# Attention's value projection: two of its four L21+L22 weight sums are added by DMA at pages 4 and 6 instead of by VectorE, and the loads and sums around them are placed anew

## The chip, the cores and the metric

The kernel runs on one core of a Trainium2 chip. The metric is the device time of one execution in microseconds (us); the median of three executions of the kernel before is 2254.22 us (2251.8 to 2255.15).

## The reference, cut to what matters

One layer of a streaming encoder on a sequence of 512 tokens of 2048 features, all in float32. What is touched here is one sixth of the input projection: the values of the attention heads, 512 x 2048 times 2048 x 1024.

```
h = rms_norm(x, norm_mix_w)
proj = h @ w_in                      # columns: q_a, k_a, v_a, q_g, k_g, v_g, r_g, gate_lr
y_a = chunked_band_attention(q_a, k_a, v_a, att_rel_bias)      # v_a: columns 2048 to 3071
y_g = rms_norm(gated_linear_attention(q_g, k_g, v_g, ...)) * silu(r_g)
x = x + concat(y_a, y_g) @ w_out
x = x + (gelu(conv(h2 @ w_ffn_up)[gate]) * conv(h2 @ w_ffn_up)[value]) @ w_ffn_down
x = x + sigmoid(h3 @ w_ple_gate) * (p @ w_ple_proj)
out = rms_norm(x, final_norm_w)
```

## The kernel before, in words

**The products.** Every large float32 product is cut in quarters and made with seven instead of eight quarter products (Strassen's scheme in Winograd's form). Each operand is split in a high part that a matmul takes whole and a low rest, and three matmuls (high x high, high x low, low x high) replace one float32 product. For the weights, a split is one ScalarE copy (the high part, `w`) and one VectorE subtraction (the low part, `w`), both of 128 x 1024.

**The values of attention** are the stage of this case. `values_product` (line 1140, called at line 1531) runs the seven products in the order P1, P2, P4, P5, P6, P3, P7, each over four weight pages j = 0 to 3 of 128 x 1024 (512 KB), so there are 28 pages, numbered n = 0 to 27. The weight operand of a page is

- pages 0 to 3: L11, 4 to 7: L12, 8 to 11: L22, each loaded as it lies in memory;
- pages 12 to 15: S1 = L21 + L22;
- pages 16 to 19: S2 = S1 + L11; pages 20 to 23: S4 = S2 + L12;
- pages 24 to 27: S3 = L21 + L11.

S1, S2 and S4 of one j are made one after the other in the same page of SBUF, named `wva_s0` to `wva_s3` in the program (`wva_s` in the profile). The pages that are loaded plainly, and those of S3, are named `wva_P..._r`: the first digit after P is the product, the second is j, so `wva_P40_r` is page 8 and `wva_P70_r` is page 24. They lie in a ring of four buffers, so page 24 takes the place of page 8, page 25 that of page 9, and so on.

**Four operations feed a page.** `value_load` (line 1112) and `sum_load` (line 1117) start a plain load from SyncE's queue, 16 and 4 of them, each 512 KB. `sum_more` (line 1121) starts a DMA from GpSimd's queue that adds a page of weights in memory onto a page in SBUF; "adding DMA" below. `sum_right` (line 1127) adds L22 onto a sum page by a VectorE instruction. `value_split` (line 1131) is the split; three buffers take its results in turn, so the split of page n + 2 is written in the program at page n and cannot begin before TensorE has left page n - 1.

**What sets the order.** At page n the program issues, in this order: the load of page n + 4 (while that is under 12), the split of page n + 2, then what the table at lines 1511 to 1522 lists for page n (`plan`), then the 12 matmuls of page n. After each product `values_collect` takes the result out of PSUM, on ScalarE or VectorE. From here on every engine and both DMA-issuing queues (SyncE's and GpSimd's) keep the order of the program (`in_order(True, True)`), so an instruction that waits holds up all that stands behind it on its engine. The other entries of the table are the last operands of this stage on the activation side (`right`, `differences`, `spread_differences`: ScalarE and VectorE), the output of the values before (`second_out`: ScalarE and GpSimd's queue), the forget gate of the linear attention (`gate_sum`, `gate_scan` on VectorE, `gate_decay` on ScalarE, `gate_small` on VectorE) and `give`, which hands a free page to the next stage, whose first weights are then loaded.

In the kernel before, L21 for the sums is loaded at pages 5 to 8, L22 is added by VectorE at pages 8 to 11, L11 by DMA at pages 11 to 14, L12 by DMA at pages 16 to 19. For S3, L21 is loaded at pages 9 to 12 and L11 added by DMA at pages 10, 15, 20 and 21.

The profile gives nearly all instructions line 64 (the helper that records them), so groups are told apart by tiles. The products' PSUM tiles are `vaA` to `vaD`: P1, P6 and P7 go to `vaA`, P2 to `vaB`, P4 to `vaD`, P5 and P3 to `vaC`.

Of the kernel before, what the change touches and what calls it, by code (L numbers as in the profile page):

```python
# [42 lines left out]
def encoder_block(ctx: ExitStack, tc: tile.TileContext, A, out):  # L43
# [1451 lines left out]
    va = dict(pages=[(p, j) for p in VALUE_ORDER for j in range(4)], raw={}, sum={}, l22={}, tiles={}, have=set())  # L1495

    def at_page(n, *fs):
        plan.setdefault(n, []).extend(fs)
# [10 lines left out]
        values_out(va["first"], 1, out_tiles, ts)  # L1509

    for n, *fs in ((0, (second_out, (0, 1)), (spread_differences, 4)),
                   (1, (second_out, (2, 3)), (right, 5), (right, 6)), (2, (differences, 5)), (3, (spread_differences, 5)), (4, (right, 7)),
                   (5, (sum_load, va, 0), (differences, 6)), (6, (sum_load, va, 1), (spread_differences, 6)),
                   (7, (sum_load, va, 2), (differences, 7)), (8, (sum_load, va, 3)), (9, (spread_differences, 7)),
                   (12, (gate_sum, (0, 1))), (13, (gate_scan, (0,))), (14, (gate_sum, (2, 3))), (15, (gate_scan, (1,))),
                   (16, (gate_scan, (2,))), (17, (gate_scan, (3,))),
                   *((8 + j, (sum_right, va, j)) for j in range(4)), *((9 + j, (value_load, va, 24 + j)) for j in range(4)),
                   *((11 + j, (sum_more, va, 16 + j, "L11")) for j in range(4)),
                   *((16 + j, (sum_more, va, 20 + j, "L12")) for j in range(4)),
                   *((i, (sum_more, va, 24 + j, "L11")) for j, i in enumerate((10, 15, 20, 21))),  # L1520
                   *((18 + i, (gate_decay, (i,))) for i in range(4)),
                   *((22 + i, (gate_small, (i,))) for i in range(4)), (26, (linear_pages,)),
                   *((n, (give, tag)) for n, tag in ((19, "r4"), (20, "r5"), (23, "r1"), (24, "r2"), (25, "r0"), (26, "r3")))):
        at_page(n, *(lambda f=f, a=a: f(*a) for f, *a in fs))
# [293 lines left out]
```

## Time and profile before

| | |
|---|---|
| three executions, median (lowest to highest) | 2254.22 us (2251.8 to 2255.15) |
| the profiled execution: its own time | 2254.77 us |
| the profiled execution: span, first to last instruction | 2253.1 us |
| mean granted TensorE clock | 0.998 |
| DMA traffic | 568.72 MB, mean 252 GB/s |

All times within the profile are microseconds from the start of the span. PE is TensorE, PEld its weight loads, DVE VectorE, ACT ScalarE, POOL GpSimd, SP SyncE; a name ending in q is an engine's queue of issues. "DMA share" is the mean busy share of the core's 16 DMA engines; it is a sum over queues and reads up to 1.06 to 1.08 when they are all busy. In a timeline the bracket at the end of a row tells how long the engine had been idle and what ended that. q1 is the DMA queue of SyncE's loads, q0 that of GpSimd's.

### The profile page before, as it was taken

How to read it: one execution, taken by the hardware profiler on the slowest of the kernel's cores; microseconds unless marked ns; L12 is line 12 of the kernel's file. 1: busy time of each engine (PE TensorE's matmuls, PEld its weight loads, DVE VectorE, ACT ScalarE, POOL GpSimd, SP SyncE). 2: the span in 40 equal slices, each digit the busy share in tenths (PEclk: the TensorE clock that was granted, in tenths of full speed). 3: DMA queues.
4: the chain of work that ended last, by engine and by line, in shares of the span. 5: the costliest groups of instructions: out<-in, count | busy, mean ns of one | idle time of the engine just before them, and what ended most of it. 6: DMA issues, size and time to landing. Idle time of an engine off the chain costs nothing.

```text
span 2253.1 us, 45666 instructions
## 1 busy us (share of the span) xinstructions
PE 2230.5 (99%) x18248; PEld 2180.2 (97%) x18248; DVE 1896.0 (84%) x2603; ACT 1321.7 (59%) x1960; POOL 199.2 (9%) x243
## 2 busy tenths in 40 slices
PE   9999999999999999999999999999999999999997
PEld 7879999999899999999999999999999999999997
DVE  6876779998688888898888888888898787898987
ACT  6654567776665665555555555555564554666765
POOL 1021111011100011111111100000000100000000
PEclk9999999999999999999999999999999999999999
DMA  5499889888978979999999987777866967879896
GB/s 206 131 238 252 223 228 241 235 229 239 355 260 246 341 211 291 289 279 285 281 265 284 260 235 209 218 208 215 263 227 220 317 212 234 309 246 335 280 296 207
DMA packets 202052, 568.72 MB, mean 252 GB/s; under 512 B 22032, under 2 KB 64272, under 8 KB 201840
## 3 DMA queue, kind: packets, MB, share of 16 engines
q1 hardware_dynamic: 168336, 448.58, 56.1%
q0 software_dynamic: 32064, 114.83, 27.2%
q8 instruction: 143, 2.34, 0.4%
q10 hardware_dynamic: 1440, 2.40, 0.3%
q14 instruction: 69, 0.57, 0.1%
HBM read 492.33 MB, written 119.54 MB: 272 GB/s over the span
## 4 chain that ended last, share of the span: by engine, by line
PE 89%; DVE 5%; DMA 3%; ACT 2%; issue 2%; POOL 0%; SPq 0%; DVEq 0%; ACTq 0%; POOLq 0%
PE accA L64 44%; PE accC L64 23%; PE accB L64 11%; PE v L64 4%; DVE w L64 2%; PE pp L64 1%; DMA wva_s<-in_w_v_a 1%; PE vaA L64 1%; PE py L64 1%; PE psc L64 1%; PE ptr L64 1%; DVE u L64 1%; PE po L64 1%; DVE s L64 1%; ACT w L64 1%
## 5 line engine op out<-in xcount | busy, mean ns | idle before, releaser
L64 PE MATMUL accA<-h,w 128*128 128x256 f32 x5088 | 628.7, 280 | 1.2 <-DVE w L64 0.7
L64 PEld LDWEIGHTS accA<-h,w 128*128 128x128 f32 x5088 | 608.9, 188 | 4.1 <-ACT u L64 1.1
L64 PE MATMUL accC<-h,w 128*128 128x256 f32 x4248 | 524.1, 280 | 0.8 <-DVE w L64 0.6
L64 DVE TENSOR_TENSOR w<-s,w 128x1024 fp32r<-128x1024 f32 (+1 forms) x381 | 457.1, 1200 | 77.7 <-ACT w L64 72.0
L64 PEld LDWEIGHTS accC<-h,w 128*128 128x128 f32 x4248 | 507.9, 188 | 1.5 <-DVE w L64 0.8
L64 ACT ACTIVATE w<-l 128x1024 fp32r<-128x1024 f32 (+1 forms) x320 | 331.8, 1038 | 186.8 <-PE accC L64 119.3
L64 DVE TENSOR_TENSOR w<-l,w 128x1024 fp32r<-128x1024 f32 (+1 forms) x320 | 382.4, 1195 | 58.1 <-ACT w L64 57.5
L64 ACT ACTIVATE w<-s 128x1024 fp32r<-128x1024 f32 (+1 forms) x381 | 394.9, 1037 | 39.1 <-DVE s L64 22.8
L64 ACT ACTIVATE u<-accA 128x256 f32<-128x256 f32 x302 | 114.4, 379 | 381.5 <-PE accA L64 381.3
L64 DVE TENSOR_TENSOR s<-s,l 128x1024 f32<-128x1024 f32 (+1 forms) x176 | 211.1, 1200 | 12.5 <-DMA s<-in_w_blk 9.3
L64 POOL DMA_DIRECT2D s<-in_w_up x84 | 74.1, 882 | 735.0 <-DMA s<-in_w_up 388.7
L64 DVE SCALAR_TENSOR_TENSOR cv<-u,cw,cv 128x511 f32<-128x511 f32 (+1 forms) x176 | 131.6, 748 | 3.1
L64 PE MATMUL accA<-up_R,w 128*128 128x256 f32 x1056 | 130.5, 280 | 0.0
L64 PE MATMUL accB<-up_R,w 128*128 128x256 f32 x1056 | 130.1, 279 | 0.0
L64 PE MATMUL accA<-up_N,w 128*128 128x256 f32 x1056 | 130.1, 279 | 0.0
L64 PEld LDWEIGHTS accA<-up_R,w 128*128 128x128 f32 x1056 | 126.1, 188 | 0.5 <-issue 0.5
L64 PEld LDWEIGHTS accB<-up_R,w 128*128 128x128 f32 x1056 | 126.1, 188 | 0.0
L64 PEld LDWEIGHTS accA<-up_N,w 128*128 128x128 f32 x1056 | 126.1, 188 | 0.0
L64 ACT ACTIVATE u<-accC 128x256 f32<-128x256 f32 x98 | 37.4, 382 | 92.0 <-PE accC L64 91.5
L64 DVE TENSOR_TENSOR u<-u,accC 128x256 f32<-128x256 f32 x102 | 42.7, 418 | 56.6 <-PE accC L64 55.4
L64 PE MATMUL v<-w,h 128*128 128x512 f32 x384 | 88.7, 391 | 0.9 <-ACT h L171 0.9
L64 PEld LDWEIGHTS v<-w,h 128*128 128x128 f32 x384 | 71.8, 188 | 16.6 <-ACT h L171 1.1
(302 smaller groups left out, 2900.2 us busy)
## 6 DMA issues: line engine op xcount, KB each, us to landing
l<-in_w_up SPq DMA_DIRECT2D x132, 512.0 KB, 6.9
s<-in_w_up SPq DMA_DIRECT2D x84, 512.0 KB, 6.0
s<-in_w_up POOLq DMA_DIRECT2D x84, 512.0 KB, 7.6
l<-in_w_dn SPq DMA_DIRECT2D x56, 448.0 KB, 5.0
l<-in_w_blk SPq DMA_DIRECT2D x48, 512.0 KB, 6.0
s<-in_w_blk SPq DMA_DIRECT2D x32, 512.0 KB, 4.6
s<-in_w_blk POOLq DMA_DIRECT2D x32, 512.0 KB, 7.8
l<-in_w_out SPq DMA_DIRECT2D x28, 512.0 KB, 4.4
```

What stands on the lines that cost most here:

```text
L64: ins = f(*args, **kw)
```

## The change

Only the table changes. Of the stage's sums:

- L22 of j = 0 and 1 is added by DMA (`sum_more` of pages 12 and 13, at pages 4 and 6) and not by VectorE; j = 2 and 3 stay on VectorE, at pages 10 and 11 as before. Two VectorE instructions go, two adding DMAs come.
- L21 for the sums is loaded at pages 1, 3, 5 and 7, not 5, 6, 7 and 8.
- L21 for S3 is loaded at pages 7, 8, 11 and 12, not 9, 10, 11 and 12.
- L11 is added onto it at pages 8, 9, 19 and 20, not 10, 15, 20 and 21.
- The adding DMAs of L12 (S4) stand at pages 15 to 18, not 16 to 19. Those of L11 for S2 stay at 11 to 14.

```diff
@@ -1509,15 +1509,17 @@
     for n, *fs in ((0, (second_out, (0, 1)), (spread_differences, 4)),
-                   (1, (second_out, (2, 3)), (right, 5), (right, 6)), (2, (differences, 5)), (3, (spread_differences, 5)), (4, (right, 7)),
-                   (5, (sum_load, va, 0), (differences, 6)), (6, (sum_load, va, 1), (spread_differences, 6)),
-                   (7, (sum_load, va, 2), (differences, 7)), (8, (sum_load, va, 3)), (9, (spread_differences, 7)),
+                   (1, (second_out, (2, 3)), (sum_load, va, 0), (right, 5), (right, 6)), (2, (differences, 5)),
+                   (3, (sum_load, va, 1), (spread_differences, 5)), (4, (right, 7), (sum_more, va, 12, "L22")),
+                   (5, (sum_load, va, 2), (differences, 6)), (6, (sum_more, va, 13, "L22"), (spread_differences, 6)),
+                   (7, (sum_load, va, 3), (differences, 7)), (9, (spread_differences, 7)),
...
-                   *((8 + j, (sum_right, va, j)) for j in range(4)), *((9 + j, (value_load, va, 24 + j)) for j in range(4)),
+                   (10, (sum_right, va, 2)), (11, (sum_right, va, 3)),
+                   *((i, (value_load, va, 24 + j)) for j, i in enumerate((7, 8, 11, 12))),
                    *((11 + j, (sum_more, va, 16 + j, "L11")) for j in range(4)),
-                   *((16 + j, (sum_more, va, 20 + j, "L12")) for j in range(4)),
-                   *((i, (sum_more, va, 24 + j, "L11")) for j, i in enumerate((10, 15, 20, 21))),
+                   *((15 + j, (sum_more, va, 20 + j, "L12")) for j in range(4)),
+                   *((i, (sum_more, va, 24 + j, "L11")) for j, i in enumerate((8, 9, 19, 20))),
```

**GpSimd's queue**, from the writes of P2's results (`vad`) on. Before, the S3 sum of page 24 stands ahead of the four sums with L11, and that of page 25 between them and the four sums with L12:

```order
L64 DMA vad_205<-pair_r6_106 128x4x128 x2
L64 DMA wva_P70_r_1198<-in_w_v_a 128x1024
L64 DMA wva_s0_1112<-in_w_v_a 128x1024
L64 DMA wva_s1_1134<-in_w_v_a 128x1024
L64 DMA wva_s2_1154<-in_w_v_a 128x1024
L64 DMA wva_s3_1178<-in_w_v_a 128x1024
L64 DMA wva_P71_r_1215<-in_w_v_a 128x1024
L64 DMA wva_s0_1112<-in_w_v_a 128x1024
```

The same place of the changed program, from two rows earlier:

```order
L64 DMA wva_s0_1033<-in_w_v_a 128x1024
L64 DMA wva_s1_1076<-in_w_v_a 128x1024
L64 DMA vad_205<-pair_r6_106 128x4x128 x2
L64 DMA wva_P70_r_1164<-in_w_v_a 128x1024
L64 DMA wva_P71_r_1184<-in_w_v_a 128x1024
L64 DMA wva_s0_1033<-in_w_v_a 128x1024
L64 DMA wva_s1_1076<-in_w_v_a 128x1024
L64 DMA wva_s2_1117<-in_w_v_a 128x1024
L64 DMA wva_s3_1158<-in_w_v_a 128x1024
L64 DMA wva_s0_1033<-in_w_v_a 128x1024
```

The two new sums stand ahead of P2's writes, and both early S3 sums stand ahead of the four sums with L11; nothing is left between these and the sums with L12. Behind the last sum with L12 come the S3 sums of pages 26 and 27 in both.

**SyncE's queue**, from the load of page 6 (`wva_P22_r`) on, before:

```order
L64 DMA wva_P22_r_1050<-in_w_v_a 128x1024
L64 DMA wva_P23_r_1070<-in_w_v_a 128x1024
L64 DMA wva_P40_r_1090<-in_w_v_a 128x1024
L64 DMA wva_P41_r_1108<-in_w_v_a 128x1024
L64 DMA wva_s0_1112<-in_w_v_a 128x1024
L64 DMA wva_P42_r_1130<-in_w_v_a 128x1024
L64 DMA wva_s1_1134<-in_w_v_a 128x1024
L64 DMA wva_P43_r_1150<-in_w_v_a 128x1024
L64 DMA wva_s2_1154<-in_w_v_a 128x1024
L64 DMA wva_s3_1178<-in_w_v_a 128x1024
L64 DMA wva_P70_r_1198<-in_w_v_a 128x1024
L64 DMA wva_P71_r_1215<-in_w_v_a 128x1024
```

And in the changed program, from the load of `wva_s0` on:

```order
L64 DMA wva_s0_1033<-in_w_v_a 128x1024
L64 DMA wva_P22_r_1052<-in_w_v_a 128x1024
L64 DMA wva_P23_r_1072<-in_w_v_a 128x1024
L64 DMA wva_s1_1076<-in_w_v_a 128x1024
L64 DMA wva_P40_r_1094<-in_w_v_a 128x1024
L64 DMA wva_P41_r_1113<-in_w_v_a 128x1024
L64 DMA wva_s2_1117<-in_w_v_a 128x1024
L64 DMA wva_P42_r_1135<-in_w_v_a 128x1024
L64 DMA wva_P43_r_1154<-in_w_v_a 128x1024
L64 DMA wva_s3_1158<-in_w_v_a 128x1024
L64 DMA wva_P70_r_1164<-in_w_v_a 128x1024
L64 DMA wva_P71_r_1184<-in_w_v_a 128x1024
```

The loads of the sum pages stand one to four places earlier. The loads of pages 24 and 25 keep their places in the row, but they now wait for VectorE's split of pages 8 and 9 alone and no longer for its sums (`sum_right` of j = 0 and 1) that read the same buffers.

**VectorE**, from the split of page 10 to that of page 14, before (a row that writes `wva_s` is a `sum_right`; `h1` is a split on the activation side):

```order
L64 TENSOR_TENSOR w_101<-wva_P42_r_1130,w_101 128x1024
L64 TENSOR_TENSOR wva_s0_1112<-wva_s0_1112,wva_P40_r_1090 128x1024
L64 TENSOR_TENSOR w_101<-wva_P43_r_1150,w_101 128x1024
L64 TENSOR_TENSOR h1_102<-pair_c0_110,h1_102 128x1024
L64 TENSOR_TENSOR wva_s1_1134<-wva_s1_1134,wva_P41_r_1108 128x1024
L64 TENSOR_TENSOR w_101<-wva_s0_1112,w_101 128x1024
L64 TENSOR_TENSOR wva_s2_1154<-wva_s2_1154,wva_P42_r_1130 128x1024
L64 TENSOR_TENSOR w_101<-wva_s1_1134,w_101 128x1024
L64 TENSOR_TENSOR wva_s3_1178<-wva_s3_1178,wva_P43_r_1150 128x1024
L64 TENSOR_TENSOR w_101<-wva_s2_1154,w_101 128x1024
```

And in the changed program:

```order
L64 TENSOR_TENSOR w_101<-wva_P42_r_1135,w_101 128x1024
L64 TENSOR_TENSOR w_101<-wva_P43_r_1154,w_101 128x1024
L64 TENSOR_TENSOR h1_102<-pair_c0_110,h1_102 128x1024
L64 TENSOR_TENSOR w_101<-wva_s0_1033,w_101 128x1024
L64 TENSOR_TENSOR wva_s2_1117<-wva_s2_1117,wva_P42_r_1135 128x1024
L64 TENSOR_TENSOR w_101<-wva_s1_1076,w_101 128x1024
L64 TENSOR_TENSOR wva_s3_1158<-wva_s3_1158,wva_P43_r_1154 128x1024
L64 TENSOR_TENSOR w_101<-wva_s2_1117,w_101 128x1024
```

Two of the four sums are gone; the rest keeps its order. The rows of TensorE and ScalarE stand as before.

## The prediction

> **What bounds the kernel now.** First the page: engines' busy time against the span.
>
> ```profile
> span 2253.1 us, 45666 instructions
> PE 2230.5 (99%) x18248; PEld 2180.2 (97%) x18248; DVE 1896.0 (84%) x2603; ACT 1321.7 (59%) x1960; POOL 199.2 (9%) x243
> ```
>
> TensorE is busy for all but 23 us, so a change can only win where TensorE waits. The second view is the timeline of PE over the values of attention: start, length, matmuls, and the wait in the bracket.
>
> ```profile
> 125.68 11.04 PE L64 MATMUL vaD<-w,h 128*128 128x512 f32 x48
> 136.56 11.04 PE L64 MATMUL vaC<-w,h 128*128 128x512 f32 x48
> 148.54 0.50 PE L64 MATMUL vaA<-w,h 128*128 128x512 f32 x1 [0.94 <-ACT w L64]
> 149.80 10.97 PE L64 MATMUL vaA<-w,h 128*128 128x512 f32 x47 [0.76 <-DVE w L64]
> 161.15 0.51 PE L64 MATMUL vaC<-w,in_R 128*128 128x512 f32 x1 [0.38 <-ACT w L64]
> ...
> 174.63 11.21 PE L64 MATMUL vaA<-w,h 128*128 128x512 f32 x48
> 185.67 2.96 PE L64 MATMUL accA<-in_R,w 128*128 128x256 f32 x24
> ```
>
> A product without waits takes 136.56 - 125.68 = 10.88 us. P6 (the first `vaA` row) should begin at 147.44 and begins at 148.54, and its second matmul comes 1.26 us after the first, not 0.23: 1.1 + 1.0 = **2.1 us lost ahead of P6**. Its other 47 matmuls should end at 160.45; P3 begins at 161.15 and takes 13.48 us: 0.7 + 2.6 = **3.3 us lost around P3**. P7 loses 0.2 more. The stage wastes 5.6 us, 0.25% of the time; that is all there is to win here.
>
> Who ends these waits? The chain of work that ended last (start, length, what), then ScalarE's timeline:
>
> ```profile
> 137.92 12.06 DMA wva_s<-in_w_v_a
> ...
> 150.04 9.89 DMA wva_s<-in_w_v_a
> ```
>
> ```profile
> 160.03 1.06 ACT L64 ACTIVATE w<-wva_s 128x1024 fp32r<-128x1024 f32 x1 [3.98 <-DMA wva_s<-in_w_v_a]
> ...
> 163.71 1.05 ACT L64 ACTIVATE w<-wva_s 128x1024 fp32r<-128x1024 f32 x1
> ...
> 166.91 1.06 ACT L64 ACTIVATE w<-wva_s 128x1024 fp32r<-128x1024 f32 x1
> ```
>
> The adding DMAs. The sum with L12 for page 20 lands at 159.93 and its split starts at 160.03; the splits of pages 21 and 22 follow 3.7 and 6.9 us later without a wait, because the forget gate's ScalarE work stands between them. So P3's three lost microseconds hang on that one landing. Why it is late shows GpSimd's timeline, and the landings of single issues in narrow windows of the DMA view (last number: us from issue to landing):
>
> ```profile
> 135.18 0.93 POOL L64 DMA_DIRECT2D wva_P_r<-in_w_v_a  x1 [5.42 <-DVE wva_s L64]
> 135.76 1.24 POOL L64 DMA_DIRECT2D wva_s<-in_w_v_a  x1
> ...
> 143.34 0.93 POOL L64 DMA_DIRECT2D wva_P_r<-in_w_v_a  x1
> ...
> 150.04 0.85 POOL L64 DMA_DIRECT2D wva_s<-in_w_v_a  x1 [5.78 <-DMA wva_s<-in_w_v_a]
> ```
>
> ```profile
> wva_P_r<-in_w_v_a POOLq DMA_DIRECT2D x1, 512.0 KB, 8.3
> wva_s<-in_w_v_a POOLq DMA_DIRECT2D x1, 512.0 KB, 11.6
> wva_P_r<-in_w_v_a SPq DMA_DIRECT2D x1, 512.0 KB, 7.7
> ...
> wva_P_r<-in_w_v_a POOLq DMA_DIRECT2D x1, 512.0 KB, 14.0
> ```
>
> Landings, issue plus length: page 24's S3 sum 143.5, the first sum with L11 147.4, page 25's S3 sum (issued 143.34) 157.3, page 20's sum 159.93. The adding DMAs land in the order of issue, 2.5 to 3.9 us apart, so page 20's sum stands in line behind page 25's, which is not needed before P7. The busy time in stretches (the last two columns are DMA share and GB/s) and two shares by queue (packets, MB, share of the engines; q1 from 112.5 to 125 us, q0 from 147.5 to 162.5 us) say how full the line is:
>
> ```profile
> 112.00:125.00 13.00, 13.00 (x60) 10.74 (x59) 12.10 (x17) 8.70 (x10) 0.00 (x0) 1.00 0.89 299
> 125.00:137.00 12.00, 12.00 (x54) 9.95 (x53) 11.90 (x15) 6.07 (x7) 3.33 (x4) 1.00 0.59 216
> 137.00:165.00 28.00, 25.17 (x107) 19.74 (x106) 17.31 (x18) 12.50 (x17) 8.66 (x11) 1.00 1.04 218
> ```
>
> ```profile
> q1 hardware_dynamic: 949, 3.46, 82.2%
> ```
>
> ```profile
> q0 software_dynamic: 870, 3.17, 106.7%
> ```
>
> From 137 to 165 us the DMA engines are full (1.04): there they, not VectorE, decide. Before that they have room. A page is 0.524 MB. A plain load occupies the engines for 12.5 x 0.822 / 6.6 pages = 1.56 us; an adding DMA for 15 x 1.067 / 6.05 pages = 2.65, or one every 2.48 us when they run alone.
>
> **The change part by part.**
>
> *Two VectorE sums go.*
>
> ```profile
> 122.06 1.22 DVE L64 TENSOR_TENSOR w<-wva_P_r,w 128x1024 fp32r<-128x1024 f32 x1
> 124.41 1.22 DVE L64 TENSOR_TENSOR w<-wva_P_r,w 128x1024 fp32r<-128x1024 f32 x1
> ...
> 129.59 1.22 DVE L64 TENSOR_TENSOR wva_s<-wva_s,wva_P_r 128x1024 f32<-128x1024 f32 x1
> ...
> 134.14 1.22 DVE L64 TENSOR_TENSOR w<-wva_s,w 128x1024 fp32r<-128x1024 f32 x1
> ```
>
> Each takes 1.22 us, and VectorE runs nearly without a break there (11.90 of 12 us). But TensorE does not wait in P2, P4 or P5 (no bracket on the rows above), so 2 x 1.2 us less is worth nothing by itself. It lets page 12's low part end about 1.5 us before today's 135.36, and the sum with L11 that waits for it could issue at 134, not 135.76. I count this at nothing, since that sum will stand in line (next step).
>
> *Two adding DMAs come, page 25's S3 sum and two loads move ahead.* SyncE's issues today:
>
> ```profile
> 112.72 3.18 SPq L64 DMA_DIRECT2D wva_P_r<-in_w_v_a  x2
> 115.95 0.43 SPq L64 DMA_DIRECT2D wva_s<-in_w_v_a  x1
> 118.72 0.33 SPq L64 DMA_DIRECT2D wva_P_r<-in_w_v_a  x1
> ...
> 120.45 0.33 SPq L64 DMA_DIRECT2D wva_P_r<-in_w_v_a  x1
> 120.82 0.91 SPq L64 DMA_DIRECT2D wva_s<-in_w_v_a  x2
> ```
>
> Afterwards page 24's load can issue when page 8's split ends (122.06 + 1.22 = 123.3) and page 25's at 125.6. In line from 112 us to the end of page 24's load stand: the loads of s1, pages 8 and 9, s2, pages 10 and 11, s3 and page 24 (8 x 1.56 = 12.5), half of page 7's and earlier writes (about 2, an estimate), and both new sums (5.3): 19.8, at 1.06 a stretch of 18.7 us. Page 24's load lands at about 131.5, page 25's 1.5 us later. The new sums themselves land before 128; they are needed when page 12 is split at about 131.4. Pages 10 and 11 land at about 127.5 and 129, for splits that reach VectorE at 128.5 and 130: 1 to 4 us later than today, still inside the lead of the split over TensorE. So I expect **no new wait in P2 to P5**.
>
> GpSimd's queue then issues page 24's S3 sum at about 132.5 to 133 (today 135.18), page 25's after it, and only then the first sum with L11. Today 12.2 us pass from the first of these issues (135.18) to the landing of the sum with L11 (147.4), with one adding DMA ahead; now two are ahead: 133 + 12.2 + 2.5 = 147.7. **P6's term: +0.3 us.** Its bounds: if the engines were never idle up to there the sum could land at 145, and P6 would lose nothing (-2.1); if both loads take as long as one that has adding DMAs beside it (9.3 us instead of 3.4, rows below) and the line in front moves at 3.9 instead of 2.5 us a sum, 150.5 (+3).
>
> ```profile
> wva_P_r<-in_w_v_a SPq DMA_DIRECT2D x2, 512.0 KB, 3.4
> ```
>
> ```profile
> wva_P_r<-in_w_v_a SPq DMA_DIRECT2D x1, 512.0 KB, 9.3
> ```
>
> Nothing then stands between the L11 sums and the L12 sums. Page 20's sum lands 159.93 - 147.4 - 2.5 = 10.0 us after the first L11 sum, not 12.5: at 157.7. Its high part is ready at 158.9, before P3 can begin (160.7). The splits of pages 21 and 22 follow by the same ScalarE intervals; page 22's low part is ready 9.2 us after page 20's split starts, at 167.0, where TensorE would want it at 166.6. **P3's term: -3.3 + 0.4 = -2.9 us.** Its bounds: 0, if that landing does not move, and -3.3.
>
> *L12's sums one page earlier in the program:* each waits for the split that reads its page and for the landing of the L11 sum, as today (the bracket 5.78); nothing.
>
> *Behind the stage.* The next stage's weights are asked for when pages of this one come free (`give`), so they shift with it:
>
> ```profile
> 185.99 1.22 DVE L64 TENSOR_TENSOR s<-s,l 128x1024 f32<-128x1024 f32 x1 [3.40 <-DMA s<-in_w_blk]
> ```
>
> ```profile
> 191.27 2.96 PE L64 MATMUL accA<-h,w 128*128 128x256 f32 x24
> ```
>
> That stage's first sum arrives at 185.99 for a product at 191.27, 5 us of cover; and GpSimd's queue, one S3 sum shorter behind P3, empties earlier. Nothing is lost there.
>
> Sum: +0.3 - 2.9 = -2.6 us. The profiled execution took 2254.77 us, 0.55 above the median of the three; it would take 2252.2, and the median goes from 2254.22 to **2251.6 us**.
>
> **The rivals.**
>
> *All of it goes.* If page 24's load lands 2.5 us earlier than I think, the L11 sum lands by 145.2 and every wait but 0.4 us is gone: -5.2, 2249.0 us. For it: 0.41 of the engines lies idle from 125 to 137. Against: the two new sums want 5.3 of it and page 25's S3 sum 2.65 more, and a sum cannot issue before its load has landed. The Trainium skill, page "DMA: Bandwidth & Descriptors", section on the anatomy of a DMA on GpSimd's path, fits such a DMA as 2.0 us plus bytes over 436 GB/s; for 512 KB the moving part would be 1.2 us, an estimate by that page, so four sums in line would end 5 us earlier and this rival would hold. The q0 row here has 2.48 us a sum, so the trace does not agree for sums.
>
> *GpSimd's queue is held by a late load.* All sums with L11 now stand behind both S3 sums, and these behind loads that share the engines with the new sums. If page 25's load (issued 125.6) needs as long as the slowest issue quoted, 14.0 us, its sum issues at 140.5, lands 8.3 later at 148.8, and the L11 sum another 2.5 to 3.9 later, 152: 4.7 us later than today. P3 gains nothing beyond its own shift if the L12 sums are 3.9 apart too: 2254.2 + 4.7 = 2258.9 us. It costs time as soon as the L11 sum lands after 150.3 (147.4 + 2.9). Against: no plain load quoted took more than 9.3. The Trainium skill, same page, section "Issuing engines are not separate DMA queues", says that DMAs of all issuers run on the same 16 engines and interleave; the trace agrees (3.4 alone, 7.7 and 9.3 beside sums), which is why I keep this case.
>
> *The gain is given back.* The stage ends earlier and TensorE waits as much longer for the next stage: 2254.2 us. Against: the 5 us of cover.
>
> **How the numbers follow.** Forecast 0.52, all goes 0.20, held queue 0.16, given back 0.12. A measurement of this kernel tells about 0.2% (4.5 us) from no change. Faster by more than that (under 2249.7): nearly all of the second case and a little of the first, 0.22. Slower by more (over 2258.7): the held queue in its worse half and mishaps of its kind, 0.11. Within: 0.67. The range takes in -5.6 us with the scatter of the medians below, and half of the way to the held queue above: 2247.5 to 2256.5.
>
> **What would show it.** Page 24's load landing near 131.5; the first L11 sum near 147.5 and P6's bracket about as today; page 25's S3 sum landing before it; page 20's sum near 157.7, P3's 48 matmuls taking 11 to 11.3 us; the next stage beginning near 183. I am wrong if a bracket appears in P2 to P5, if GpSimd waits past 134 for a load, or if P6's wait vanishes.

## The result, and the profile after

The changed kernel takes 2249.33 us, the median of 22 runs (2247.66 to 2253.81), against 2252.44 us of the kernel before beside it (22 runs, 2249.82 to 2260.73). The ratio is 0.9985 with a 95% interval of 0.9978 to 0.9991: a gain of 3.4 us, between 2.0 and 5.0. The 3.4 lie inside the 0.2% that the prediction counted as no change. The profiled execution took 2248.59 us.

The page, engines' busy time against the span:

```profile
span 2246.8 us, 45663 instructions
PE 2228.0 (99%) x18248; PEld 2178.3 (97%) x18248; DVE 1893.9 (84%) x2601; ACT 1321.4 (59%) x1960; POOL 201.2 (9%) x245
```

VectorE has its two instructions less and is 2.1 us less busy. That lies within the interval of the gain, so these numbers alone do not say whether it is VectorE's time that came back; number 5 below does. PE over the stage (start, length, matmuls, wait):

```profile
103.98 11.04 PE L64 MATMUL vaA<-w,in_R 128*128 128x512 f32 x48
...
136.62 11.04 PE L64 MATMUL vaC<-w,h 128*128 128x512 f32 x48
147.50 0.46 PE L64 MATMUL vaA<-w,h 128*128 128x512 f32 x1
148.73 10.95 PE L64 MATMUL vaA<-w,h 128*128 128x512 f32 x47 [0.76 <-DVE w L64]
159.51 5.96 PE L64 MATMUL vaC<-w,in_R 128*128 128x512 f32 x25
165.66 5.51 PE L64 MATMUL vaC<-w,in_R 128*128 128x512 f32 x23 [0.19 <-DVE w L64]
171.00 11.21 PE L64 MATMUL vaA<-w,h 128*128 128x512 f32 x48
182.05 2.96 PE L64 MATMUL accA<-in_R,w 128*128 128x256 f32 x24
```

With 10.88 us for a product without waits, P6 begins on time (136.62 + 10.88 = 147.50) and loses 1.0 us behind its first matmul; before it lost 2.1. Then 0.13 us pass ahead of P3, and P3 takes 171.00 - 159.51 = 11.49 us, 0.61 too long; together 0.74, before 3.3. From the stage's first matmul to the next stage's first, 78.07 us pass. The kernel before has 103.92 and 185.67 there, so 81.75: the stage is **3.7 us** shorter. Its first row, in the kernel before:

```profile
103.92 11.04 PE L64 MATMUL vaA<-w,in_R 128*128 128x512 f32 x48
```

(The two profiled spans stand 6.3 us apart. Matching the matmuls of the two traces one by one, another 1.4 us come between about 565 and 630 us, and 2.6 between about 1680 and 1990, with the same instructions. In that last stretch numbers 1, 3 and 4 below are as slow as the kernel before and the other seven as fast as the change, so this change does not decide it.)

GpSimd's queue (start, length, wait) and the landings of single issues in narrow windows of the DMA view (last number: us from issue to landing), in the order page 24's load, page 25's load, page 24's S3 sum, the first sum with L11, page 20's sum:

```profile
132.24 0.92 POOL L64 DMA_DIRECT2D wva_P_r<-in_w_v_a  x1 [2.13 <-ACT h L64]
133.57 0.91 POOL L64 DMA_DIRECT2D wva_P_r<-in_w_v_a  x1 [0.42 <-issue]
134.15 1.23 POOL L64 DMA_DIRECT2D wva_s<-in_w_v_a  x1
...
148.97 0.86 POOL L64 DMA_DIRECT2D wva_s<-in_w_v_a  x1 [5.84 <-DMA wva_s<-in_w_v_a]
```

```profile
wva_P_r<-in_w_v_a SPq DMA_DIRECT2D x1, 512.0 KB, 7.9
...
wva_P_r<-in_w_v_a SPq DMA_DIRECT2D x1, 512.0 KB, 6.8
...
wva_P_r<-in_w_v_a POOLq DMA_DIRECT2D x1, 512.0 KB, 5.4
...
wva_s<-in_w_v_a POOLq DMA_DIRECT2D x1, 512.0 KB, 12.1
...
wva_s<-in_w_v_a POOLq DMA_DIRECT2D x1, 512.0 KB, 7.3
```

The loads are issued at 123.69 and 125.96 and land at 131.6 and 132.8. The first S3 sum lands at 132.24 + 5.4 = 137.6, the first sum with L11 at 134.15 + 12.1 = 146.25, page 20's at 148.97 + 7.3 = 156.3. Busy time in stretches (last two columns: DMA share, GB/s):

```profile
112.00:125.00 13.00, 13.00 (x59) 10.78 (x58) 11.86 (x17) 8.59 (x10) 0.87 (x1) 1.00 1.03 307
125.00:137.00 12.00, 12.00 (x54) 9.94 (x54) 11.31 (x14) 5.99 (x7) 4.42 (x6) 1.00 0.92 309
137.00:165.00 28.00, 27.24 (x120) 21.99 (x119) 17.85 (x18) 16.13 (x24) 7.66 (x9) 1.00 1.06 230
```

The share went from 0.89 to 1.03 and from 0.59 to 0.92: 0.14 x 13 + 0.33 x 12 = 5.8 us of all engines' time that lay idle before are now used. By queue, q0's share goes from 5.9% to 45.7% and from 10.8% to 38.8%, so the adding DMAs take 8.5 us more of the engines' time in these 25 us, and the plain loads 2.7 less. Whether the gain comes from there, the experiments ask.

### The profile page after: what moved, and what is told of

It reads as the page before. It is cut to its first block, busy times and chain, and to the rows that moved or that the text cites. A ratio compares the mean times of both kernels' runs of the same rounds, so it can differ in the third digit from the quotient of the medians.

```text
span 2246.8 us, 45663 instructions
## 1 busy us (share of the span) xinstructions
PE 2228.0 (99%) x18248; PEld 2178.3 (97%) x18248; DVE 1893.9 (84%) x2601; ACT 1321.4 (59%) x1960; POOL 201.2 (9%) x245
## 4 chain that ended last, share of the span: by engine, by line
PE 86%; DVE 5%; DMA 5%; ACT 2%; issue 2%; POOL 0%; SPq 0%; ACTq 0%; DVEq 0%; POOLq 0%
PE accA L64 44%; PE accC L64 22%; PE accB L64 11%; PE v L64 4%; DVE w L64 2%; DMA l<-in_w_ple_gate 1%; PE py L64 1%; DMA wva_s<-in_w_v_a 1%; DMA s<-in_w_blk 1%; PE psc L64 1%; PE ptr L64 1%; ACT w L64 1%; PE po L64 1%; DVE u L64 0%; DVE s L64 0%
```

## The experiments

**Theory A**: TensorE's waits are set by the line of adding DMAs on GpSimd's queue, about one per 2.5 us; what counts is how many stand ahead of the sum that is needed, and whether they run in time in which the DMA engines were idle. **Theory B**, the rival: it is VectorE's 2.4 us. Each kernel was compared with the kernel before on the same chip (medians of before 2252.4 to 2253.1 us). "Stage" runs from the first matmul of P1 to the first of the next stage; 28 pages of 2.72 us, so 76.2 us, is a stage without a wait.

| kernel | median us | ratio (95% interval) | stage us | first L11 sum lands | page 20's lands |
|---|---|---|---|---|---|
| before (first profile) | 2252.44 | | 81.75 | 147.4 | 159.9 |
| the change | 2249.33 | 0.9985 (0.9978 to 0.9991) | 78.07 | 146.3 | 156.3 |
| 1: before, page 25's sum late | 2251.07 | 0.9991 (0.9982 to 0.9999) | 79.38 | 146.7 | 158.0 |
| 2: before, all S3 sums late | 2251.10 | 0.9993 (0.9985 to 1.0002) | 77.78 | 143.6 | 154.9 |
| 3: the two L22 sums alone | 2248.85 | 0.9982 (0.9974 to 0.9991) | 77.80 | 142.0 | 155.9 |
| 4: the new places alone | 2255.75 | 1.0010 (1.0001 to 1.0018) | 83.59 | 150.7 | 160.6 |
| 5: VectorE's time given back | 2250.84 | 0.9986 (0.9978 to 0.9995) | 77.94 | 144.8 | 156.1 |
| 6: change, page 25's sum late | 2246.47 | 0.9972 (0.9960 to 0.9983) | 76.32 | 142.3 | 153.7 |
| 7: change, all S3 sums late | 2248.93 | 0.9983 (0.9974 to 0.9991) | 76.32 | 142.9 | 154.4 |
| 8: all four L22 sums by DMA | 2252.36 | 0.9999 (0.9991 to 1.0008) | 82.88 | 150.2 | 160.1 |
| 9: the change again | 2249.65 | 0.9988 (0.9979 to 0.9997) | 78.13 | 145.7 | 156.2 |
| 10: number 6 again | 2246.45 | 0.9977 (0.9968 to 0.9986) | 76.32 | 142.2 | 153.5 |

### 1 and 2: the S3 sums out of the way, in the kernel before

Number 1 moves one adding DMA (page 25's S3 sum) behind the sums with L12; number 2 moves page 24's as well. Nothing on VectorE changes.

```diff
-                   *((i, (sum_more, va, 24 + j, "L11")) for j, i in enumerate((10, 15, 20, 21))),
+                   *((i, (sum_more, va, 24 + j, "L11")) for j, i in enumerate((10, 19, 20, 21))),
```

(number 2: `(19, 19, 20, 21)`)

> The kernel before, with one number changed: the S3 sum of page 25 is issued behind the four L12 sums (page 19) and no longer ahead of them (page 15). Theory A (the line of adding DMAs): the first L11 sum lands as before, near 147.4, so P6 loses about 2.1 us as before; page 20's sum has one adding DMA less ahead and lands near 157.4 instead of 159.9; the stage, from the first matmul of P1 to the first of the next stage, takes 78.8 us instead of 81.75; 2.8 us faster than before. Theory B (VectorE's time): VectorE does the same work, so nothing changes.

> The kernel before, with all four S3 sums behind the L12 sums (pages 19, 19, 20, 21); all L22 sums stay on VectorE. Theory A: nothing is ahead of the first L11 sum, which lands near 145 instead of 147.4, page 20's sum lands near 155; P6 loses 0.5 us or less, P3 0.4; the stage takes 77.0 us, 4.8 us faster than before, more than the change itself gains. Theory B: nothing changes.

PE in number 1:

```profile
147.92 0.44 PE L64 MATMUL vaA<-w,h 128*128 128x512 f32 x1
...
161.01 6.19 PE L64 MATMUL vaC<-w,in_R 128*128 128x512 f32 x25
...
172.74 11.21 PE L64 MATMUL vaA<-w,h 128*128 128x512 f32 x48
```

P3 takes 172.74 - 161.01 = 11.73 us and starts 161.01 - 147.92 - 10.88 = 2.2 us late: P6's loss is as before (2.1), P3's falls from 3.3 to 0.85. One adding DMA less in front of page 20's sum was worth 2.45 us. In number 2 P6 loses nothing, as both sums are gone from the line; P7 now waits 0.6 us for its own late sums and takes 12.23 us to the next stage's first matmul instead of 11.04, so the stage takes 77.78, not 77.0. Both are A's result: the stage gained 2.4 and 4.0 us with VectorE untouched. The medians gained 2.0 us each, and the interval of number 2 takes in no change: part of the gain is given back in the next stage (numbers 6 and 7).

### 3 and 4: each half of the change alone

Number 3 is the kernel before with the two L22 sums by DMA (and the loads that they need) and nothing else moved; number 4 is the change with all four L22 sums left on VectorE, so that only the order is new. The first diff is against the kernel before, the second against the change.

```diff
-                   (1, (second_out, (2, 3)), (right, 5), (right, 6)), (2, (differences, 5)), (3, (spread_differences, 5)), (4, (right, 7)),
-                   (5, (sum_load, va, 0), (differences, 6)), (6, (sum_load, va, 1), (spread_differences, 6)),
+                   (1, (second_out, (2, 3)), (sum_load, va, 0), (right, 5), (right, 6)), (2, (differences, 5)),
+                   (3, (sum_load, va, 1), (spread_differences, 5)), (4, (right, 7), (sum_more, va, 12, "L22")),
+                   (5, (differences, 6)), (6, (sum_more, va, 13, "L22"), (spread_differences, 6)),
...
-                   *((8 + j, (sum_right, va, j)) for j in range(4)), *((9 + j, (value_load, va, 24 + j)) for j in range(4)),
+                   *((8 + j, (sum_right, va, j)) for j in (2, 3)), *((9 + j, (value_load, va, 24 + j)) for j in range(4)),
```

```diff
-                   (3, (sum_load, va, 1), (spread_differences, 5)), (4, (right, 7), (sum_more, va, 12, "L22")),
-                   (5, (sum_load, va, 2), (differences, 6)), (6, (sum_more, va, 13, "L22"), (spread_differences, 6)),
+                   (3, (sum_load, va, 1), (spread_differences, 5)), (4, (right, 7)),
+                   (5, (sum_load, va, 2), (differences, 6)), (6, (spread_differences, 6)),
...
-                   (10, (sum_right, va, 2)), (11, (sum_right, va, 3)),
-                   *((i, (value_load, va, 24 + j)) for j, i in enumerate((7, 8, 11, 12))),
+                   *((8 + j, (sum_right, va, j)) for j in range(4)),
+                   *((i, (value_load, va, 24 + j)) for j, i in enumerate((8, 9, 11, 12))),
```

> One part of the change alone: the two L22 sums by DMA at pages 4 and 6 with their two loads at pages 1 and 3; the S3 sums stay where they are before (pages 10, 15, 20, 21), their loads too. Theory A: page 24's load issues near 126 and lands near 132, its sum issues near 132.3, and the first L11 sum, with that one ahead, lands near 142 to 143.5, page 20's near 154.5; the stage takes 76.8 us, 4.9 us faster than before and 1.2 faster than the change. Theory B: two VectorE instructions less as in the change, so the same as the change, 78.1 us.

> The other part alone: the order of the changed kernel on GpSimd's queue (the S3 sums of pages 24 and 25 at pages 8 and 9 ahead of the L11 sums, the L12 sums at pages 15 to 18, loads of the sum pages early), but all four L22 sums on VectorE at pages 8 to 11 as before, so the loads of pages 24 and 25 wait for them again (pages 8 and 9). Theory A: page 25's load lands near 137.6, its sum issues at 138.5 and holds the first L11 sum, which lands near 149.5 to 150; P6 loses 4 to 4.5 us, P3 0.5; the stage takes 80.8 to 81.3, 0.5 to 1 us faster than before. Theory B: VectorE has the work of before, so 81.75, no change.

PE in number 3, then PE and GpSimd's queue in number 4:

```profile
147.40 11.04 PE L64 MATMUL vaA<-w,h 128*128 128x512 f32 x48
158.28 3.18 PE L64 MATMUL vaC<-w,in_R 128*128 128x512 f32 x13
...
170.63 11.20 PE L64 MATMUL vaA<-w,h 128*128 128x512 f32 x48
```

```profile
136.76 11.04 PE L64 MATMUL vaC<-w,h 128*128 128x512 f32 x48
151.87 0.80 PE L64 MATMUL vaA<-w,h 128*128 128x512 f32 x1 [4.07 <-ACT w L64]
153.13 12.82 PE L64 MATMUL vaA<-w,h 128*128 128x512 f32 x47 [0.47 <-DVE w L64]
165.78 11.04 PE L64 MATMUL vaC<-w,in_R 128*128 128x512 f32 x48
```

```profile
135.25 0.93 POOL L64 DMA_DIRECT2D wva_P_r<-in_w_v_a  x1 [5.29 <-DVE wva_s L64]
138.72 0.87 POOL L64 DMA_DIRECT2D wva_P_r<-in_w_v_a  x1 [2.54 <-ACT w L64]
139.29 2.96 POOL L64 DMA_DIRECT2D wva_s<-in_w_v_a  x3
```

Number 3 has the whole gain: P6 loses nothing, P3 170.63 - 158.28 - 10.88 = 1.5 us (a stage of 76.8 was expected; page 25's sum still lands just ahead of page 20's, at 153.5 and 155.9). The order alone costs time. While VectorE still adds L22, it releases the buffers of pages 8 and 9 late, page 25's load comes late, and its sum, now ahead of all sums with L11, holds GpSimd's queue to 138.72: three sums with L11 then issue at once, and the first lands at 150.7. TensorE waits 4.07 us. So the two L22 sums on the DMA side do two things: they run in idle DMA time, and they let page 24's load start early: it is issued at 123.4 in number 3, at 131.1 in number 4. No run has the early load with these two sums still on VectorE, so that the load is what gains is shown by exclusion (number 5) and not by a run of its own. I had expected 80.8 to 81.3 us for number 4 and got 83.6; 1.9 of the rest is a fall of the clock, shown under the last heading.

### 5: VectorE's time given back

The change, with the low part of pages 11 and 12 computed twice: two VectorE instructions of 1.2 us more, about where the two sums used to stand.

```diff
+            if n in (11, 12):
+                vec.tensor_tensor(lo, raw, hi.bitcast(F32), ALU.subtract)
```

> The changed kernel with VectorE's time put back: the subtractions for the low parts of pages 11 and 12 are done twice (the same result again), 2 x 1.2 us at about the places where the two L22 sums stood. Theory A: the first L11 sum waits until 135 for page 12's split but still stands behind page 25's sum, and lands near 146.3 as in the change; the stage takes 78.1 to 78.4 us, 3.3 us faster than before. Theory B: the gain goes, 80.5 us or more.

```profile
147.37 3.11 PE L64 MATMUL vaA<-w,h 128*128 128x512 f32 x13
151.07 8.25 PE L64 MATMUL vaA<-w,h 128*128 128x512 f32 x35 [0.59 <-DVE w L64]
159.16 6.05 PE L64 MATMUL vaC<-w,in_R 128*128 128x512 f32 x25
```

P6 loses 159.16 - 147.37 - 10.88 = 0.9 us, as in the change, and the stage takes 77.94. **Theory B falls**: with VectorE as busy as before (1896.8 us, 1896.0 in the kernel before), the gain stays. The two loads issue early here too (123.3 and 125.6 us, against 131.1 and 134.5 in number 4, whose VectorE has nearly the same work and whose stage is 5.6 us longer, 1.9 of it by the clock).

### 6 and 7: the S3 sums out of the way, in the change

```diff
-                   *((i, (sum_more, va, 24 + j, "L11")) for j, i in enumerate((8, 9, 19, 20))),
+                   *((i, (sum_more, va, 24 + j, "L11")) for j, i in enumerate((8, 18, 19, 20))),
```

(number 7: `(18, 18, 19, 20)`)

> The changed kernel with the S3 sum of page 25 behind the L12 sums (page 18) instead of at page 9. Theory A: the first L11 sum has one adding DMA less ahead and lands near 143.8 instead of 146.25, page 20's sum near 154; P6 and P3 lose 0.3 us together; the stage takes 76.6 us, 5.1 us faster than before and 1.5 faster than the change. Theory B: VectorE's work is that of the change, 78.1 us.

> The changed kernel with both early S3 sums (pages 24 and 25) behind the L12 sums (page 18). Theory A: the first L11 sum lands near 141 to 142, no wait is left, the stage takes 76.4 us, 5.3 us faster than before, no more than 0.2 beyond the variant with page 25 alone late. Theory B: 78.1 us.

Both stages are without a wait (76.32, for P7 takes 11.04 us to the next stage's first matmul here, not 10.88), so page 25's sum ahead of the sums with L11 cost the change its last 1.75 us. Yet number 7 is no faster than the change. Its next stage, against the change's (`pat` is a product of the linear attention there):

```profile
205.52 1.21 PE L64 MATMUL accB<-in_R,w 128*128 128x256 f32 x8 [0.34 <-DVE w L64]
...
211.66 1.16 PE L64 MATMUL pat<-g_t,g_t 128*128 128x128 f32 x8 [1.69 <-DVE g_t L64]
```

```profile
211.55 1.16 PE L64 MATMUL pat<-g_t,g_t 128*128 128x128 f32 x8 [0.89 <-DVE g_t L64]
```

From the next stage's first matmul to this one pass 31.20 us in number 7 (from 180.46), 29.50 in the change (from 182.05). Number 7 began 1.6 us sooner and is there no sooner. Four S3 sums stand behind its sums with L12, and the next stage's first adding DMA, which waits for a load that shares the engines with them, issues at 176.19, in the change at 174.41, although the stage ends sooner; it lands at 182.1 in both. That these sums cause the delay is read from the traces and was not tested. The rival "the gain is given back" exists, then, but not in the change; numbers 1 and 2 show it too, with 30.5 and 30.6 us (before 29.27, from 185.67 to 214.94). Number 5 has 30.1, not far outside the scatter: two executions of the change have 29.5 and 29.1, two of number 6's kernel 28.9 and 29.4. The time from P1's first matmul to `pat` takes in what is given back, and it orders the kernels nearly as their medians do: 112.6 us in number 4, 111.3 in 8, 111.0 before, 109.9 in 1, 108.4 in 2, 108.0 in 5, 107.6 in the change, 107.5 in 7, 106.8 in 3, 105.2 in 6.

### 8: all four L22 sums by DMA

```diff
-                   (7, (sum_load, va, 3), (differences, 7)), (9, (spread_differences, 7)),
+                   (7, (sum_load, va, 3), (differences, 7)), (8, (sum_more, va, 14, "L22")),
+                   (9, (sum_more, va, 15, "L22"), (spread_differences, 7)),
...
-                   (10, (sum_right, va, 2)), (11, (sum_right, va, 3)),
```

> The change, with the last two L22 sums also added by DMA (pages 14 and 15, at pages 8 and 9, each ahead of the S3 sum of its page); VectorE does none. Theory A (the line of adding DMAs decides): the two new sums stand ahead of the sums with L11 and want 2 x 2.48 = 5.0 us of the engines, of which about 2 us lay idle in the change between 112 and 137 us (share 0.92 and 1.03). So the first sum with L11 lands 3 to 5 us later than the change's 146.25, at 149.3 to 151.3, P6 waits 4 to 6 us ahead of and behind its first matmul, and the stage takes 81 to 83 us (change 78.07). Median 2252 to 2255. Theory B (VectorE's time decides): 2.4 us less on VectorE is worth up to the 1.85 us of waits that the change has left, stage 76.2 to 77.5, median 2247 to 2249.

```profile
136.74 5.83 PE L64 MATMUL vaC<-w,h 128*128 128x512 f32 x25
...
146.43 0.50 PE L64 MATMUL vaC<-w,h 128*128 128x512 f32 x1 [0.83 <-ACT w L64]
147.69 2.79 PE L64 MATMUL vaC<-w,h 128*128 128x512 f32 x11 [0.76 <-DVE w L64]
151.38 0.50 PE L64 MATMUL vaA<-w,h 128*128 128x512 f32 x1 [0.90 <-ACT w L64]
152.64 12.58 PE L64 MATMUL vaA<-w,h 128*128 128x512 f32 x47 [0.76 <-DVE w L64]
165.05 11.04 PE L64 MATMUL vaC<-w,in_R 128*128 128x512 f32 x48
```

VectorE does 2.4 us less still, and the stage is 4.8 us longer than in the change: A again, in the range forecast (81 to 83). The waits stand in P5, not only in P6 as I had written: P5 starts at 136.74 and P6 14.64 us later, because page 15's new sum lands only at 145.2, behind page 24's S3 sum. Of the 4.8 us, 1.6 are a fall of the clock (last heading), 3.2 longer waits. The idle DMA time was mostly spent with two sums; the third and fourth, at the places that they have here, are paid for in waits. Other places for them were not tried.

### 9 and 10: the change and number 6 side by side

> The change once more, beside the next run on the same chip. Ratio to before 0.9985 within 0.0008, median about 2249.4; stage 78.1, first sum with L11 landing near 146.3, so that these rows are shown to return from one execution to another. Both theories expect the same.

> The change with page 25's S3 sum at page 18, once more, beside the change on the same chip. Theory A: stage 76.3, and 1.7 us less than the change from the stage, 2247.5 to 2248, ratio to before 0.9975 to 0.9978. Theory B (VectorE's work is that of the change): as the change, 2249.4. A gain of 2.9 us, as the two single results stood apart, would be more than the stage explains.

PE in number 10:

```profile
147.42 11.04 PE L64 MATMUL vaA<-w,h 128*128 128x512 f32 x48
158.30 11.04 PE L64 MATMUL vaC<-w,in_R 128*128 128x512 f32 x48
169.18 11.21 PE L64 MATMUL vaA<-w,h 128*128 128x512 f32 x48
180.23 2.97 PE L64 MATMUL accA<-in_R,w 128*128 128x256 f32 x24
```

The rows return: stages of 78.13 and 76.32 (78.07 and 76.32 the first time). One S3 sum goes first, while the DMA engines are not yet full (a share of 0.92 in number 6, from its issue at 132.15 to its landing at 137.72), then the sums with L11 and L12, then three S3 sums; no wait is left in the stage. This version beats both kernels: 2246.5 us in both sets, 6.2 to 6.6 us under the kernel before. Against the change the medians stand 3.2 us apart here and 2.9 the first time. The stage explains 1.8 of it, and the profiled spans of numbers 9 and 10 stand 1.9 apart (2246.2 and 2244.3); the rest is inside the intervals and not traced to a place.

## Why the prediction was right, point by point

- **P3's term (-2.9 us): right.** It measured 0.74 - 3.3 = -2.6. Page 20's sum was to land 10.0 us behind the first sum with L11 and landed 10.05 behind it, at 156.3 (157.7 was forecast, with the later first sum), so it no longer decides. P3 takes 11.49 us, a little over the 11 to 11.3 that were to show it; the 0.61 too many stand mostly at page 22. There 0.4 had been left, and the working should have given 0.6: with P3 beginning at 160.7, page 22's second matmul comes 25 matmuls of 0.227 us later, at 166.4 and not 166.6. Number 1 shows the cause by itself: page 25's sum taken out of the line, -2.45 us.
- **P6's term (+0.3 us): mis-sized, it was -1.1.** The mechanism was as written: page 25's sum lands ahead of the first sum with L11 and costs it time, as number 6 shows by removing it. The step that failed was to take before's 12.2 us, from the issue of page 24's sum to the landing of the first sum with L11, as it stood for a queue whose first sum finds idler engines: while page 24's sum is under way the DMA share is 0.81 in the change and 0.96 before, and the sum takes 5.4 us, not 8.3. In numbers 6 and 10, where it alone stands ahead, that stretch takes 10.1 and 10.4 us (142.27 - 132.15 in number 6). The 2.5 us for page 25's sum were too few (the upper bound had 3.9): with both ahead the stretch takes 14.0 us in the change and 13.7 in number 9, so that sum costs 3.3 to 3.9. The two errors partly cancel, and that is luck; 12.2 + 2.5 = 14.7 was forecast for the 14.0. GpSimd's queue also began at 132.24, not 133. So the landing came at 146.25 instead of 147.7, and the bracket ahead of P6's first matmul went; the one behind it stayed (0.76 us). The prediction had named "P6's wait vanishes" as a sign of being wrong, and half of it did.
- **No wait in P2 to P5: right**, though the cover was thinner on ScalarE than the brackets on PE show. Page 10's split waits for its load:

```profile
127.61 1.07 ACT L64 ACTIVATE w<-wva_P_r 128x1024 fp32r<-128x1024 f32 x1 [3.21 <-DMA wva_P_r<-in_w_v_a]
```

- **VectorE's two instructions worth nothing by themselves: right** (number 5). But the sentence missed what the missing instructions release. It is in the next step, as page 24's load at 123.3, and numbers 3, 4 and 5 together point to it as the heart of the matter.
- **Page 24's load near 131.5: right** (131.6), and page 25's "1.5 us later" was 1.2. The count of the line by engine time, 1.56 us a load and 2.65 a sum, came near: as written it ends at 112 + 18.7 = 130.7, and nothing in it gives the 0.8 us up to 131.5.
- **The sum**: -2.6 us was forecast. The stage measures -3.7, 1.4 more than forecast from P6's term and 0.3 less from P3's; the medians give -3.1 and the ratio -3.4, with an interval (-2.0 to -5.0) that takes in the -2.6.
- **The rivals.** "All of it goes" would need page 24's load 2.5 us sooner; it came as forecast, and what went beyond the forecast came from the queue behind it. Number 6 reaches this rival's stage by another route. "The held queue" needed a load of 14.0 us; the change's took 6.8, and number 4 shows the case made real, at a late start of the load rather than a long one. "Given back" is not in the change (29.50 against 29.27 us to `pat`) and is clearly in numbers 1, 2 and 7. The rule of the Trainium skill that was weighed, 2.0 us plus bytes over 436 GB/s (page "DMA: Bandwidth & Descriptors", section "Anatomy of one DMA — SWDGE (gpsimd) path"), would have such sums end 1.2 us apart, an estimate by that page; in the changed kernel the sums of pages 16 to 22 land 2.45 to 2.6 us apart, so the trace again goes by the q0 row.

## What to carry to other kernels

Where a queue of adding DMAs feeds the critical engine, order it by when each result is needed, and look for the stretch in which the DMA engines are idle: work moved there can be free up to the idle time and is paid for in waits beyond it (two sums there gained 4.0 us of stage in number 3, two more cost 4.8 at the places tried). An instruction on an engine that nobody waits for can still be worth moving if it is the last reader of a buffer: look at what its end releases. And when one stage has been smoothed, look in the next stage for the work that was pushed behind it.

## What the runs showed of the hardware

**The clock fell after one long wait and after several short ones, and that adds to them.** Single microseconds of number 4 and of number 8 (columns: busy time by engine, granted TensorE clock, DMA share, GB/s):

```profile
150.00:151.00 1.00, 0.00 (x0) 0.00 (x0) 0.00 (x0) 0.24 (x1) 0.00 (x0) 0.68 1.09 217
...
156.00:157.00 1.00, 1.00 (x4) 0.81 (x3) 0.93 (x2) 0.71 (x1) 0.69 (x1) 0.50 1.07 209
157.00:158.00 1.00, 1.00 (x5) 0.79 (x5) 1.00 (x2) 0.00 (x0) 0.00 (x0) 0.90 1.01 201
```

```profile
152.00:153.00 1.00, 0.36 (x1) 0.36 (x2) 1.00 (x2) 0.25 (x1) 0.12 (x1) 0.83 1.09 217
...
156.00:157.00 1.00, 1.00 (x5) 0.83 (x5) 0.86 (x2) 0.31 (x1) 0.22 (x1) 0.96 1.07 213
```

In number 4 the clock drops to 0.50 some 2.6 us into the wait that began at 147.8 and comes back at about 157.2, four microseconds after P6's second matmul; P6's 47 matmuls take 165.78 - 153.13 = 12.65 us from their start to P3's, where the change needs 159.51 - 148.73 = 10.78. A wait of 4.07 us (and the 0.47 behind the first matmul) thus cost 1.9 more. The Trainium skill, page "TensorE: Matmul & The Clock Gate", section "Why this matters for your kernels", warns of idle gaps over about 3 us. Number 4 agrees; number 8 goes further, since no single bracket there is over 0.90 us, and the clock was halved all the same, from about 152.7 to 156.1, after four of 0.76 to 0.90 within some 7 us (P6's 47 matmuls take 165.05 - 152.64 = 12.41 us, so 1.6 are lost). The waits of the kernel before, 0.94 and 0.76, left it at 1.00 (147 to 153 us). How much waiting it takes, these runs do not show. The expectations for both kernels left this out.

**A plain load beside adding DMAs shares bytes evenly, not time.** One stretch, the change's DMA view from 139 to 146 us (packets, MB, share of the engines; q0 the sums, q1 the loads):

```profile
q0 software_dynamic: 263, 0.95, 68.9%
q1 hardware_dynamic: 245, 0.88, 36.6%
```

Both queues move nearly the same number of bytes, and the sums take almost twice the engine time for them. The kernel before agrees in the same stretch (0.90 and 0.89 MB, 65.6% and 35.5%). It fits this that loads of 3.4 us alone take 7.9 and 9.1 beside sums in the change, and that sums with a load beside them land 4.8 and 3.9 us behind the one before, not 2.5.
